# A delta-rule recurrence on one core: the block inverse widened ahead of the value stage, a third RH tile, and 64-row products that alternate between heads

## The chip, the cores and the metric

The kernel runs on 1 of the 8 cores of a Trainium2 chip. The metric is the device time of one execution in microseconds (us). Below, PE is TensorE, DVE is VectorE, ACT is ScalarE, POOL is GpSimd, and SP is SyncE, whose queue issues nearly all DMAs here.

## The reference

One layer of a hybrid decoder trunk, sequence 1024, width 1024. After an RMS norm one projection feeds three mixers: stick-breaking attention (8 heads of 64), a Mamba-2 SSD mixer (16 heads of 64, chunks of 128) and RWKV-7 time mixing (8 heads of 64). Their gated outputs are projected, merged and added to the input. The change lies in the third mixer, whose state `S` (64 x 64 for each head) is stepped through the tokens as

```
sa = S @ (-kk_t)
S  = S * w_t + outer(sa, kk_t * a_t) + outer(v_t, k_t)
y_t = S @ r_t
```

The kernel computes it in chunks of 64 tokens. In each chunk the steps are turned into products of small matrices and one inverse of a unit lower triangular 64 x 64 matrix for each head.

## The kernel before, in words

Everything that PE does is written out in one order by a small planner (`Driver`, lines 69 to 131). It keeps a clock of its own that every product advances by a fixed cost (`Counted`, lines 50 to 66), and at each step it takes the first of the small generators whose yielded pause is over, whose condition holds and whose PSUM banks the plan holds to be free; where there is none, it issues the next piece of a long projection (`proj`, line 243: 24 groups of three fp32r products `pj` of 128x512, hi and lo parts, each with its weights). Projections that nothing waits for, those of the merge gates, are `spare`: they fill PE's time wherever the recurrence or the SSD chunks have nothing ready, but the last four (`KEEP`) are held back for the time after the SSD chunks. PE then runs that list strictly in order. The order on the other engines is made by the framework's scheduler.

`rwkv()` (line 385) goes through 4 pairs of heads. For a pair, `prep` (line 457) makes for each half of the sequence (512 tokens) the decayed vectors: `KR` (keys and receptances) and `BK` (the two factors they are multiplied with). `mats` (line 530) then runs one unit, which is 256 tokens of both heads of the pair, so there are 16 units, `u` = 0 to 15, two to a half. A unit goes through these stages:

- keys: 8 products `pma<-KR,BK` (line 546), each with 64 rows of contraction, in the upper or the lower half of the partitions according to the head; DVE masks them into the tile `RH` (line 548); 4 transposes of `BK` (line 555) complete it;
- a 16 x 16 inverse on DVE for 32 small blocks at once: `RH` goes to DRAM (`dC`, line 563) and comes back as `CB` (line 567); 30 short operations (lines 571 and 573); then out to DRAM as `img` (line 578) and back as the block diagonal tiles `Ta` and `Tb` (line 579);
- value stage (lines 591 to 606): centred values and transposed keys, then 64x64 products with the two heads in opposite quarters of the array;
- widening of the inverse from 16 to 32 (lines 613 to 623: products `Ta,C`, a copy on ACT to `U`, products `Tb,tmp`, a subtraction on DVE to `T32`);
- solving (lines 626 to 642: `X,T`, `tmp,C`, `tmp,T`), operators `Z` (lines 645 to 657), four state steps (line 666) in which a unit needs the state that the unit before leaves, and the normalised output.

What holds a unit back: `mats` starts when `u - 2` has its operators (line 534); the value stage starts when `u - 1` has them (line 590); the widening waits until the plan's clock stands `INV` past the end of the keys stage (line 612). `RH`, `Ta`, `Tb` and `BK` have two buffers each, `T32` one.

Behind the recurrence come the SSD chunks (`ssd()`, line 735). Two groups of 8 chunks are a chain: `first(c)` makes two decay products (`DH,lsr` and `DL,lsr`), from which ACT and DVE make `Mt`; after a pause of `SLOT` in the plan, in which projections fill PE, `second(c)` uses `Mt` (line 975). Then come the attention rows, the output projections and the final norm.

Of the kernel before, what the change touches and what calls it, by code (L numbers as in the profile page):

```python
# [8 lines left out]
F32 = mybir.dt.float32  # L9
# [6 lines left out]
P = 128  # L16
# [7 lines left out]
EXPM05 = 0.6065306597126334  # L24
BKB = 2
TAB = 2
# [5 lines left out]
SLOT = 5.6  # L32
INV = 24.0
LAT = 2.0
# [104 lines left out]
def body_(tc, A, out):  # L139
    nc = tc.nc  # L140
    ctx = ExitStack()
    V, G, T, ACT = nc.vector, nc.gpsimd, Counted(nc.tensor), nc.scalar
    drv = Driver(T)
    tt, ts, stt = V.tensor_tensor, V.tensor_scalar, V.scalar_tensor_tensor
    MUL, ADD, SUB = ALU.mult, ALU.add, ALU.subtract
# [8 lines left out]
    def pm(tag="a", hold=0.0):  # L154
        drv.bank(tag, hold)
        return psm.tile([P, HB], F32, name="pm" + tag)
# [210 lines left out]
    for k in range(KT):  # L367
        ps = pm("cab"[k % 3])
# [16 lines left out]
    def rwkv():  # L385
        rc = ExitStack()
        cc = rc.enter_context(tc.tile_pool(name="rcc", bufs=1))
        pr = rc.enter_context(tc.tile_pool(name="rpr", bufs=1))
        ma = rc.enter_context(tc.tile_pool(name="rma", bufs=1))
# [63 lines left out]
        fl = lambda t: t.rearrange("p b l -> p (b l)")  # L453

        ends, opst = {}, [0.0]

        def prep(hp, hf, rT, kT, vT):
# [6 lines left out]
            aa = pr.tile([P, HB], F32, name="aa")  # L464
            ps = pm("a", 2.4)
            T.matmul(ps, lhsT=wup[0:64, cs], rhs=lo[0:64, hs], start=True, stop=True)
            ACT.activation(out=fl(sg), in_=ps, func=AF.Sigmoid, bias=par("rw_w0", hp))
            ps = pm("a", 2.4)
# [26 lines left out]
            V.tensor_copy(out=ivb, in_=inv.rearrange("p (c h) -> p c h", h=2).unsqueeze(3).broadcast_to([P, 4, 2, 64]))  # L495
            yield 4.5, None, "a"
            ips = pm("a", 2.4)
# [8 lines left out]
            KR = pr.tile([P, 4, 4, 64], F32, name="KR", bufs=2)  # L506
            BK = pr.tile([P, 4, 4, 64], F32, name="BK", bufs=BKB)
# [22 lines left out]
        def mats(hp, hf, g):  # L530


            u = 4 * hp + 2 * hf + g
            yield 0.0, lambda: (hp, hf) in made and T.t >= after[hp, hf] and (u < 2 or u - 2 in ends), "a"
            KR, BK, GL, bv, vs = made[hp, hf]
            a0 = 2 * g
            RH = ma.tile([P, 2, 2, 6, 64], F32, name="RH", bufs=2)
            for h in range(2):
                if h:
                    yield 0.0, None, "a"  # L540
                hr = slice(64 * h, 64 * h + 64)
                ps = pm("a", 2.6)
                pv = ps.rearrange("p (a e x) -> p a e x", a=2, e=2)
                for i in range(2):
                    for e in range(2):
                        T.matmul(pv[:, i, e, :], lhsT=fl(BK[hr, a0 + i, 2 * e:2 * e + 2, :]), rhs=KR[hr, a0 + i, e::2, :],
                                 start=True, stop=True)
                tt(out=RH[:, :, h, 1:5, :].rearrange("p a (e b) l -> p a e (b l)", e=2), in0=pv,
                   in1=fl(msk).unsqueeze(1).unsqueeze(1).broadcast_to([P, 2, 2, P]), op=MUL)
            yield 2.0, None, "b"  # L550
            ps = pm("b", 2.0)
            pv = ps.rearrange("p (a e h l) -> p a e h l", a=2, e=2, h=2)
            for i in range(2):
                for e in range(2):
                    T.transpose(out=ps[:, (2 * i + e) * P:(2 * i + e + 1) * P], in_=fl(BK[:, a0 + i, 2 - 2 * e:4 - 2 * e, :]),
                                identity=ident)
            for i in range(2):
                ACT.copy(out=RH[:, i, :, 0::5, :].rearrange("p h e l -> p e h l"), in_=pv[:, i])
# [15 lines left out]
            V.tensor_copy(out=TX, in_=TB.rearrange("q t j -> q j t"))  # L574
            Ta = ma.tile([P, 4, P], F32, name="Ta", bufs=TAB)
            Tb = ma.tile([P, 4, P], F32, name="Tb", bufs=TAB)
# [6 lines left out]
            for e in range(2):  # L583
                for (cx, mx) in ((C16, m16), (C32, m32)):
                    tt(out=cx[:, :, e, :], in0=RHg[:, :, 2 + 2 * e, :],
                       in1=mx[:, 64 * e:64 * e + 64].unsqueeze(1).broadcast_to([P, 4, 64]), op=MUL)
            f = lambda t, i: fl(t[:, i])

            t0_ = T.t
            yield 2.0, lambda: u == 0 or u - 1 in ends and T.t >= opst[0] + 1.0, "aa"  # L590
# [16 lines left out]

            def tmp():
                return ma.tile([P, 4, P], F32, name="tmp", bufs=2)


            yield max(2.0, INV - (T.t - t0_))
            ups = pm("b")
            for q in range(4):
                T.matmul(ups[:, q * P:(q + 1) * P], lhsT=f(C16, q), rhs=Ta[:, q, :], start=True, stop=True)
            U = tmp()
            ACT.copy(out=fl(U), in_=ups)
            yield LAT
            ups = pm("b")
            for q in range(4):  # L620
                T.matmul(ups[:, q * P:(q + 1) * P], lhsT=U[:, q, :], rhs=Tb[:, q, :], start=True, stop=True)
            T32 = ma.tile([P, 4, P], F32, name="T32")
            tt(out=fl(T32), in0=fl(Tb), in1=ups, op=SUB)

# [49 lines left out]
            for h in range(2):  # L674
                yv = yb[h][:, 0:256].rearrange("p (a e l) -> p a e l", e=2, l=64)
                ACT.copy(out=Yt[0:64, :, h, :], in_=yv[0:64, :, 0, :])
                ACT.copy(out=Yt[64:128, :, h, :], in_=yv[64:128, :, 1, :])
            Yq = ma.tile([P, 4, 64], F32, name="Yq", bufs=2)
            Yt3 = Yt.rearrange("p a h l -> p (a h) l")
# [12 lines left out]
            for i in range(2):  # L692
                T.transpose(out=ps[:, i * P:(i + 1) * P], in_=fl(Yq[:, 2 * i:2 * i + 2, :]), identity=ident)
            yo = pr.tile([P, 256], F32, name="yo", bufs=2)
            t0 = hf * HB + g * 256
# [641 lines left out]
```

## Time and profile before

| what | us |
|---|---|
| median of 3 runs (1584.92 to 1587.72) | 1586.35 |
| the profiled execution | 1585.81 |
| its span in the trace | 1584.1 |
| PE busy | 1546.7 (98%) |
| DVE busy | 966.4 (61%) |
| ACT busy | 724.8 (46%) |
| POOL busy | 214.6 (14%) |

The mean granted PE clock is 0.998 of full speed. A busy time of PE is made of modelled ends, and the records of products that follow each other overlap; so the price of a group of products is read here from the start of its first record to the start of the next group. Each fp32 product leaves two records (a product of 128x128 is two records of 128x128), each fp32r product and each transpose one. Order lists count a product once.

### The profile page before, as it was taken

How to read it: one execution, taken by the hardware profiler on the slowest of the kernel's cores; microseconds unless marked ns; L12 is line 12 of the kernel's file. 1: busy time of each engine (PE TensorE's matmuls, PEld its weight loads, DVE VectorE, ACT ScalarE, POOL GpSimd, SP SyncE). 2: the span in 40 equal slices, each digit the busy share in tenths (PEclk: the TensorE clock that was granted, in tenths of full speed). 3: DMA queues.
4: the chain of work that ended last, by engine and by line, in shares of the span. 5: the costliest groups of instructions: out<-in, count | busy, mean ns of one | idle time of the engine just before them, and what ended most of it. 6: DMA issues, size and time to landing. Idle time of an engine off the chain costs nothing.

```text
span 1584.1 us, 22681 instructions
## 1 busy us (share of the span) xinstructions
PE 1546.7 (98%) x8590; PEld 1256.2 (79%) x8590; DVE 966.4 (61%) x1982; ACT 724.8 (46%) x1212; POOL 214.6 (14%) x321
## 2 busy tenths in 40 slices
PE   7999999999999999999999999999999999999998
PEld 5878877887888788778777777887888778778887
DVE  5375776657567673366987934346574787555623
ACT  6263465546345554454545533246454655321211
POOL 1000000000000000201564620112121311000000
PEclk9999999999999999999999999999999999999999
DMA  4323223122222323201111113511211164886322
GB/s 161 87 61 76 58 78 84 41 62 55 72 56 73 91 51 91 73 27 40 41 41 40 28 41 100 186 44 34 62 34 46 33 207 140 279 287 225 110 107 80
DMA packets 189581, 138.72 MB, mean 88 GB/s; under 512 B 42545, under 2 KB 156320, under 8 KB 189472
## 3 DMA queue, kind: packets, MB, share of 16 engines
q1 hardware_dynamic: 189328, 137.02, 29.0%
q8 instruction: 67, 1.10, 0.3%
q14 instruction: 42, 0.34, 0.1%
q10 hardware_dynamic: 144, 0.26, 0.0%
HBM read 99.50 MB, written 37.75 MB: 87 GB/s over the span
## 4 chain that ended last, share of the span: by engine, by line
PE 80%; DVE 8%; ACT 5%; DMA 4%; issue 2%; SPq 0%; POOL 0%; POOLq 0%; DVEq 0%; ACTq 0%
PE pj L62 51%; PE pmb L62 9%; PE pma L62 9%; PE pmc L62 8%; PE pmb L66 2%; DMA yt<-in_w_o_dram 1%; PE pma L66 1%; DVE wlo L194 1%; DVE kp L1137 1%; ACT whi L193 1%; DVE TX L571 1%; DVE TB L573 1%; DMA yt<-yssd 1%; DMA yt<-ys 1%; DMA wraw<-in_w_in_dram 1%
## 5 line engine op out<-in xcount | busy, mean ns | idle before, releaser
L62 PE MATMUL pj<-hL,whi 128*128 128x512 f32 x1456 | 554.5, 397 | 0.5 <-DVE mo L1219 0.5
L62 PE MATMUL pj<-hH,whi 128*128 128x512 f32 x1328 | 540.4, 415 | 3.3 <-DVE sg L1222 2.2
L62 PE MATMUL pj<-hH,wlo 128*128 128x512 f32 x1264 | 500.3, 396 | 0.5 <-DVE wlo L194 0.5
L62 PEld LDWEIGHTS pj<-hL,whi 128*128 128x128 f32 x1456 | 273.5, 189 | 56.1 <-issue 2.1
L62 PEld LDWEIGHTS pj<-hH,whi 128*128 128x128 f32 x1328 | 250.1, 189 | 64.0 <-issue 8.2
L62 PEld LDWEIGHTS pj<-hH,wlo 128*128 128x128 f32 x1264 | 238.0, 188 | 58.3 <-DVE wlo L194 1.0
L194 DVE TENSOR_TENSOR wlo<-wraw,whi 128x1024 fp32r<-128x1024 f32 x91 | 112.3, 1234 | 153.7 <-ACT whi L193 148.9
L193 ACT CAST whi<-wraw 128x1024 fp32r<-128x1024 f32 x91 | 95.5, 1049 | 182.3 <-PE pj L62 165.6
L1137 DVE TENSOR_TENSOR_SCAN kp<-kp,one 128x127 f32<-128x127 f32 (+7 forms) x64 | 87.8, 1372 | 50.1 <-POOL kp L1135 50.0
L1156 ACT COPY aT<-pmb 128x512 f32<-128x512 f32 (+1 forms) x80 | 41.4, 547 | 57.2 <-PE pmb L66 57.0
L668 DVE TENSOR_SCALAR HI<-pmc,GL 64x64 f32<-64x64 f32 x128 | 32.5, 281 | 55.2 <-PE pmc L62 54.1
L568 POOL TENSOR_SCALAR TB<-id 32x256 f32<-32x256 f32 x16 | 14.8, 924 | 354.0 <-DMA img<-TB 245.1
L1135 POOL TENSOR_SCALAR_AFFINE_SELECT be<-be 128x128 f32<-128x128 f32 x64 | 29.8, 466 | 212.1 <-ACT be L1132 211.7
L1139 DVE TENSOR_TENSOR be<-be,kp 128x127 f32<-128x127 f32 (+7 forms) x64 | 50.0, 781 | 2.8
L62 PE MATMUL pj<-hL,wlo 128*128 128x512 f32 x128 | 50.5, 395 | 0.0
L571 DVE TENSOR_TENSOR TX<-CB,TB 32x15 f32<-32x15 f32 (+7 forms) x240 | 46.3, 193 | 6.7 <-DMA CB<-dC 0.8
L573 DVE TENSOR_TENSOR TB<-TB,TX 32x15 f32<-32x15 f32 (+7 forms) x240 | 46.3, 193 | 6.0
L939 POOL TENSOR_TENSOR DL<-li,d 128x512 fp32r<-128x512 f32 x32 | 45.5, 1434 | 25.5 <-DVE d L855 19.0
L62 PEld LDWEIGHTS pmc<-aT,vt 128*64 128x64 f32 x576 | 30.7, 136 | 16.9 <-ACT kp L1133 6.1
L62 PE MATMUL pmc<-aT,vt 128*64 128x128 f32 x576 | 38.8, 279 | 4.9 <-ACT kp L1133 3.4
L62 PEld LDWEIGHTS pmc<-HI,Z 128*128 128x128 f32 x256 | 37.3, 190 | 7.9 <-ACT Z L657 2.8
L772 DVE SCALAR_TENSOR_TENSOR yc<-pj,pc,yc 128x511 f32<-128x511 f32 (+2 forms) x48 | 35.7, 743 | 8.5 <-ACT yc L770 7.9
(380 smaller groups left out, 2635.7 us busy)
## 6 DMA issues: line engine op xcount, KB each, us to landing
wraw<-in_w_in_dram SPq DMA_DIRECT2D x75, 512.0 KB
sgd<-sgt SPq DMA_DIRECT2D x48, 256.0 KB
sg<-sgd SPq DMA_DIRECT2D x48, 256.0 KB
mg<-mo SPq DMA_DIRECT2D x32, 256.0 KB
mo<-mg SPq DMA_DIRECT2D x32, 256.0 KB
xt<-in_x_dram SPq DMA_DIRECT2D x8, 512.0 KB
Ta<-img SPq DMA_DIRECT2D x16, 256.0 KB
Tb<-img SPq DMA_DIRECT2D x16, 256.0 KB
```

The lines of the kernel that those rows point to most:

```text
L62: return self.eng.matmul(out, lhsT=lhsT, rhs=rhs, **kw)
L66: return self.eng.transpose(**kw)
L193: ACT.copy(out=hi, in_=raw)
L194: tt(out=lo, in0=raw, in1=hi.bitcast(F32), op=SUB)
L571: tt(out=TX[:, j + 1:16, 0:j + 1], in0=CB[:, j, j + 1:16].unsqueeze(2).broadcast_to(sh), in1=TB[:, j:j + 1, 0:j + 1].broadcast_to(sh), op=MUL)
L573: tt(out=TB[:, j + 1:16, 0:j + 1], in0=TB[:, j + 1:16, 0:j + 1], in1=TX[:, j + 1:16, 0:j + 1], op=SUB)
L668: ts(out=HIs[h][cur[h]][0:64, :], in0=o[hr], scalar1=GL[hr, 4 * g + c, h:h + 1], scalar2=None, op0=MUL)
L772: stt(out=o[:, d:], in0=ps[:, 0:HB - d], scalar=w(3 - d), in1=o[:, d:], op0=MUL, op1=ADD)
L939: G.tensor_tensor(out=DL, in0=lb, in1=dal[:, c, h0:h0 + 4].unsqueeze(2).broadcast_to([P, 4, P]), op=MUL)
L1137: V.tensor_tensor_scan(out=kp[:, n - 1:0:-1], data0=kp[:, n - 1:0:-1], data1=one.broadcast_to([P, n - 1]), initial=1.0, op0=MUL, op1=MUL)
L1139: tt(out=be[:, 0:n - 1], in0=be[:, 0:n - 1], in1=kp[:, 1:n], op=MUL)
L1156: ACT.copy(out=aT[:, 0:2 * m, :].rearrange("p x t -> p (x t)"), in_=ps[:, :2 * m * P])
```

## The change

- `BK` has one buffer instead of two. `prep` now waits, before it writes `BK`, until the transposes of the unit before are in the plan (`turned`).
- `RH` has three buffers, and keys may be made when `u - 3` has its operators, one unit sooner.
- The 8 products of the keys stage are written in another order: for each of the four blocks, head 0 and then head 1, into two PSUM banks taken together. The plan's clock is set back by 0.9 behind them.
- The widening stands ahead of the value stage, so it no longer waits for unit `u - 1`; its pause `INV` is 29 instead of 24. `Ta` has one buffer instead of two, `T32` two instead of one.
- `Yq` and `yo` have one buffer instead of two.

No operation is added or removed.

```
-BKB = 2
+BKB = 1
-INV = 24.0
+INV = 29.0
...
-            yield 4.5, None, "a"
+            yield 4.5, lambda: 4 * hp + 2 * hf == 0 or 4 * hp + 2 * hf - 1 in turned, "a"
...
-            yield 0.0, lambda: (hp, hf) in made and T.t >= after[hp, hf] and (u < 2 or u - 2 in ends), "a"
+            yield 0.0, lambda: (hp, hf) in made and T.t >= after[hp, hf] and (u < 3 or u - 3 in ends), "aa"
...
-            RH = ma.tile([P, 2, 2, 6, 64], F32, name="RH", bufs=2)
+            RH = ma.tile([P, 2, 2, 6, 64], F32, name="RH", bufs=3)
+            pvs = [pm("a", 2.8 + 0.7 * h).rearrange("p (a e x) -> p a e x", a=2, e=2) for h in range(2)]
+            for i in range(2):
+                for e in range(2):
+                    for h in range(2):
+                        hr = slice(64 * h, 64 * h + 64)
+                        T.matmul(pvs[h][:, i, e, :], lhsT=fl(BK[hr, a0 + i, 2 * e:2 * e + 2, :]), rhs=KR[hr, a0 + i, e::2, :],
+                                 start=True, stop=True)
+            T.t -= 0.9
             for h in range(2):
-                if h:
-                    yield 0.0, None, "a"
-                hr = slice(64 * h, 64 * h + 64)
-                ps = pm("a", 2.6)
...
+            turned.add(u)
...
-            Ta = ma.tile([P, 4, P], F32, name="Ta", bufs=TAB)
+            Ta = ma.tile([P, 4, P], F32, name="Ta", bufs=1)
...
+            yield INV, None, "b"
+            ups = pm("b", 2.0)
+            for q in range(4):
+                T.matmul(ups[:, q * P:(q + 1) * P], lhsT=f(C16, q), rhs=Ta[:, q, :], start=True, stop=True)
+            U = tmp()
+            ACT.copy(out=fl(U), in_=ups)
+            yield LAT, None, "b"
...
+            T32 = ma.tile([P, 4, P], F32, name="T32", bufs=2)
+            tt(out=fl(T32), in0=fl(Tb), in1=ups, op=SUB)
             yield 2.0, lambda: u == 0 or u - 1 in ends and T.t >= opst[0] + 1.0, "aa"
...
-            yield max(2.0, INV - (T.t - t0_))
...
-            Yq = ma.tile([P, 4, 64], F32, name="Yq", bufs=2)
+            Yq = ma.tile([P, 4, 64], F32, name="Yq")
...
-            yo = pr.tile([P, 256], F32, name="yo", bufs=2)
+            yo = pr.tile([P, 256], F32, name="yo")
```

Two places show how the lists of the engines move. The first is where the inverses of units 0 and 1 come back. On SP, before: the `img` writes of unit 1 (names `img_447`, `img_448`) and the loads of its `Ta` and `Tb`, with what each waits for.

```order
51 L578 DMA img_447<-TB 32x16x16 [waits DMAHW5_49,DVE_49,Pool_49]
52 L578 DMA img_448<-TX 32x16x16 [waits DMAHW6_49,DVE_49]
53 L579 DMA Ta<-img_447 128x4x128 [waits DMAHW5_49]
54 L579 DMA Tb<-img_448 128x4x128 [waits DMAHW6_49]
55 L192 DMA wraw<-in_w_in_dram 128x8x128 [waits DMAHW3_49,DMAHW1_49,DVE_49]
```

On SP, now:

```order
54 L580 DMA img_447<-TB 32x16x16 [waits DVE_49,Pool_49]
55 L580 DMA img_448<-TX 32x16x16 [waits DMAHW1_49,DVE_49]
56 L192 DMA wraw<-in_w_in_dram 128x8x128 [waits DMAHW2_49,DVE_49]
57 L581 DMA Ta<-img_447 128x4x128 [waits DMAHW3_49,DMAHW0_49,PE_49]
58 L581 DMA Tb<-img_448 128x4x128 [waits DMAHW4_49,DMAHW1_49]
59 L580 DMA img_445<-TB 32x16x16 [waits DVE_49,Pool_49]
```

The load of unit 1's `Ta` now waits for PE, and the `Tb` load and the next unit's `img` write stand behind it. On PE, before: the first widening product `Ta,C` of unit 0 and the rows up to its second one, `Tb,tmp`, with nine projection products between; unit 1's `Ta,C` comes 104 rows on.

```order
469 L62 MATMUL pmb<-Ta,C_973 128x128 x4
470 L62 MATMUL pj<-hH,whi 128x512
471 L62 MATMUL pj<-hL,whi 128x512
472 L62 MATMUL pj<-hH,wlo 128x512
473 L62 MATMUL pj<-hH,whi 128x512
474 L62 MATMUL pj<-hL,whi 128x512
475 L62 MATMUL pj<-hH,wlo 128x512
476 L62 MATMUL pj<-hH,whi 128x512
477 L62 MATMUL pj<-hL,whi 128x512
478 L62 MATMUL pj<-hH,wlo 128x512
479 L62 MATMUL pmb<-Tb,tmp 128x128 x4
```

On PE, now, from `Ta,C` of unit 0 (`C_982`) to that of unit 1 (`C_1071`):

```order
492 L62 MATMUL pmb<-Ta,C_982 128x128 x4
493 L62 MATMUL pj<-hH,whi 128x512
494 L62 MATMUL pj<-hL,whi 128x512
495 L62 MATMUL pj<-hH,wlo 128x512
496 L62 MATMUL pj<-hH,whi 128x512
497 L62 MATMUL pj<-hL,whi 128x512
498 L62 MATMUL pj<-hH,wlo 128x512
499 L62 MATMUL pj<-hH,whi 128x512
500 L62 MATMUL pj<-hL,whi 128x512
501 L62 MATMUL pj<-hH,wlo 128x512
502 L62 MATMUL pmb<-Tb,tmp 128x128 x4
503 L62 MATMUL pmb<-Ta,C_1071 128x128 x4
```

The second widening begins right behind the first, with nine projection products and `Tb,tmp` between the two reads of the one `Ta` buffer. The second place is the end of the SSD chunks. On PE, before: from the decay products of the last chunk but one to those of the last, 27 projection products lie ahead of the `EAx` row; here are the last rows of that filler, `second(6)`, `first(7)` and the beginning of `second(7)`.

```order
3241 L62 MATMUL pj<-hH,wlo 128x512
3242 L62 MATMUL pmb<-EAx,sel 128x512
3243 L62 MATMUL pmc<-cT,St_6278 128x128 x4
3244 L62 MATMUL pmc<-xw,bt 128x512
3245 L62 MATMUL pma<-Mt,xd 64x128 x8
3246 L62 MATMUL pma<-cT,bz_6280 128x128
3247 L62 MATMUL pmb<-DH,lsr 128x512
3248 L62 MATMUL pmb<-DL,lsr 128x512
3249 L62 MATMUL pmb<-DH,lsr 128x512
3250 L62 MATMUL pmb<-DL,lsr 128x512
3251 L62 MATMUL pj<-hH,whi 128x512
```

On PE, now, from the end of `first(6)` to that of `first(7)`:

```order
3242 L62 MATMUL pmb<-DL,lsr 128x512
3243 L62 MATMUL pmb<-EAx,sel 128x512
3244 L62 MATMUL pmc<-cT,St_6340 128x128 x4
3245 L62 MATMUL pmc<-xw,bt 128x512
3246 L62 MATMUL pma<-Mt,xd 64x128 x8
3247 L62 MATMUL pma<-cT,bz_6342 128x128
3248 L62 MATMUL pmb<-DH,lsr 128x512
3249 L62 MATMUL pmb<-DL,lsr 128x512
3250 L62 MATMUL pmb<-DH,lsr 128x512
3251 L62 MATMUL pmb<-DL,lsr 128x512
3252 L62 MATMUL pmb<-EAx,sel 128x512
```

No projection product stands in the last two chunks any more. On DVE, now, what stands there from the last chunk but one on (`yc` is the addition of a chunk's output, `St` the state):

```order
1457 L978 TENSOR_TENSOR yc<-pma,yc 128x4x128
1458 L973 TENSOR_TENSOR St_6340<-St_6340,pmc 64x512
1459 L947 TENSOR_TENSOR cb<-pma,li 128x128
1460 L948 TENSOR_TENSOR xd<-xt,dt 128x512
1461 L951 TENSOR_TENSOR Mt<-Mt,cb 128x512
1462 L939 TENSOR_TENSOR DH<-li,dah 128x512
1463 L951 TENSOR_TENSOR Mt<-Mt,cb 128x512
```

On DVE, before, the same stretch:

```order
1471 L971 TENSOR_TENSOR St_6278<-St_6278,pmc 64x512
1472 L977 TENSOR_TENSOR yc<-pma,yc 128x4x128
1473 L946 TENSOR_TENSOR cb<-pma,li 128x128
1474 L950 TENSOR_TENSOR Mt<-Mt,cb 128x512
1475 L194 TENSOR_TENSOR wlo<-wraw,whi 128x1024
1476 L950 TENSOR_TENSOR Mt<-Mt,cb 128x512
```

The last `DH`, which PE's second pair of decay products needs, now stands between the two `Mt`.

## Rows read from the trace of the kernel before

**Rows 1.** The page, part 1: busy us (share of the span) xinstructions of each engine.

```profile
PE 1546.7 (98%) x8590; PEld 1256.2 (79%) x8590; DVE 966.4 (61%) x1982; ACT 724.8 (46%) x1212; POOL 214.6 (14%) x321
```

**Rows 2.** Windows: stretch and length; PE, PEld, DVE, ACT, POOL busy; granted clock; DMA.

```profile
100.00:640.00 540.00, 528.65 (x3291) 444.43 (x3292) 351.83 (x1111) 270.41 (x450) 15.75 (x27) 1.00 0.26 68
```

**Rows 3.** Groups by form, 100 to 700 us: xrecords | busy us, mean ns | idle before.

```profile
L62 PE MATMUL pma<-KR,BK 64*128 64x128 f32 x256 | 28.6, 285 | 0.2 <-ACT sg L467 0.2
```

**Rows 4.** Timeline of PE, one keys stage and what follows: start, us, what, records.

```profile
385.01 1.71 PE L62 MATMUL pma<-KR,BK 64*128 64x128 f32 x16
386.64 0.50 PE L62 MATMUL pj<-hH,whi 128*128 128x512 f32 x1
```

**Rows 5.** Timeline of PE: 64-row products in both halves; one full 128-row product.

```profile
99.86 1.13 PE L62 MATMUL pma<-lo,wup 64*128 64x512 f32 x4
100.92 0.50 PE L62 MATMUL pj<-hH,whi 128*128 128x512 f32 x1
...
395.27 1.02 PE L62 MATMUL pma<-kp,bo 128*128 128x512 f32 x2
396.22 0.27 PE L62 MATMUL pma<-ZLe,RH 64*64 64x64 f32 x1
```

**Rows 6.** Timeline of PE: 64x64 products in opposite quarters of the array.

```profile
396.32 0.22 PE L62 MATMUL pma<-ZLe,RH 64*64 64x64 f32 x1
396.33 0.22 PE L62 MATMUL pma<-ZLo,RH 64*64 64x64 f32 x1
396.38 0.22 PE L62 MATMUL pma<-ZLe,RH 64*64 64x64 f32 x1
```

**Rows 7.** Timeline of PE: short products with full weights; products alternating between output halves.

```profile
429.63 0.55 PE L62 MATMUL pmc<-HI,Z 128*128 128x64 f32 x4
430.00 0.48 PE L62 MATMUL pj<-hH,whi 128*128 128x512 f32 x1
...
902.09 1.09 PE L62 MATMUL pma<-Mt,xd 128*64 128x128 f32 x16
903.12 0.49 PE L62 MATMUL pma<-cT,bz 128*128 128x128 f32 x2
```

**Rows 8.** Chain of waits, a Ta load from issue to landing: start, us, what.

```profile
197.91 2.83 DMA Ta<-img
```

**Rows 9.** Timeline of PE: unit 9's BK transposes.

```profile
389.28 0.60 PE L66 MATMUL pmb<-ident,BK 128*128 128x128 f32 x4
```

**Rows 10.** Timeline of SP: unit 9's Ta load is issued.

```profile
416.86 0.38 SPq L579 DMA_DIRECT2D Ta<-img  x1
```

**Rows 11.** Timeline of PE: nine projection products and a widening product.

```profile
409.64 0.48 PE L62 MATMUL pj<-hH,whi 128*128 128x512 f32 x1
...
411.83 1.05 PE L62 MATMUL pmb<-Tb,tmp 128*128 128x128 f32 x8
412.64 0.48 PE L62 MATMUL pj<-hH,whi 128*128 128x512 f32 x1
```

**Rows 12.** Chain of waits, filler of the last two SSD chunks.

```profile
904.55 6.29 PE pj L62 x27
...
915.21 0.47 PE pj L62 x2
```

**Rows 13.** Timeline of PE, last SSD chunk: [idle before <-releaser].

```profile
918.68 0.66 PE L62 MATMUL pma<-Mt,xd 128*64 128x128 f32 x8 [0.98 <-DVE Mt L950]
```

**Rows 14.** Timeline of DVE, SSD chunks.

```profile
885.26 0.78 DVE L947 TENSOR_TENSOR xd<-xt,dt 128x512 f32<-128x512 f32 x1
...
898.23 1.28 DVE L950 TENSOR_TENSOR Mt<-Mt,cb 128x512 f32<-128x512 f32 x2
...
905.63 0.68 DVE L938 TENSOR_TENSOR DH<-li,dah 128x512 fp32r<-128x512 f32 x1
...
914.29 0.69 DVE L977 TENSOR_TENSOR yc<-pma,yc 128x512 f32<-128x512 f32 x1
914.90 0.28 DVE L946 TENSOR_TENSOR cb<-pma,li 128x128 f32<-128x128 f32 x1
```

More of the change, by code (lines that the diff above doesn't have):

```diff
@@ L453, in rwkv @@
         fl = lambda t: t.rearrange("p b l -> p (b l)")
-        ends, opst = {}, [0.0]
+        ends, opst, turned = {}, [0.0], set()
         def prep(hp, hf, rT, kT, vT):
@@ L533, in mats @@
             u = 4 * hp + 2 * hf + g
-            yield 0.0, lambda: (hp, hf) in made and T.t >= after[hp, hf] and (u < 2 or u - 2 in ends), "a"
+            yield 0.0, lambda: (hp, hf) in made and T.t >= after[hp, hf] and (u < 3 or u - 3 in ends), "aa"
             KR, BK, GL, bv, vs = made[hp, hf]
             a0 = 2 * g
-            RH = ma.tile([P, 2, 2, 6, 64], F32, name="RH", bufs=2)
-            for h in range(2):
-                if h:
-                    yield 0.0, None, "a"
-                hr = slice(64 * h, 64 * h + 64)
-                ps = pm("a", 2.6)
[L543 to L547, printed above, removed]
+            RH = ma.tile([P, 2, 2, 6, 64], F32, name="RH", bufs=3)
[7 more added lines that the diff above has]
+            T.t -= 0.9
+            for h in range(2):
+                pv = pvs[h]
                 tt(out=RH[:, :, h, 1:5, :].rearrange("p a (e b) l -> p a e (b l)", e=2), in0=pv,
                    in1=fl(msk).unsqueeze(1).unsqueeze(1).broadcast_to([P, 2, 2, P]), op=MUL)
-            yield 2.0, None, "b"
+            yield 1.5, None, "b"
             ps = pm("b", 2.0)
@@ L587, in mats, with tmp @@
             f = lambda t, i: fl(t[:, i])
-            t0_ = T.t
+            def tmp():
+                return ma.tile([P, 4, P], F32, name="tmp", bufs=2)
+            yield INV, None, "b"
[5 more added lines that the diff above has]
+            yield LAT, None, "b"
+            ups = pm("b", 2.2)
+            for q in range(4):
+                T.matmul(ups[:, q * P:(q + 1) * P], lhsT=U[:, q, :], rhs=Tb[:, q, :], start=True, stop=True)
+            T32 = ma.tile([P, 4, P], F32, name="T32", bufs=2)
+            tt(out=fl(T32), in0=fl(Tb), in1=ups, op=SUB)
             yield 2.0, lambda: u == 0 or u - 1 in ends and T.t >= opst[0] + 1.0, "aa"
@@ L606, in mats @@
             ACT.copy(out=X.rearrange("p q k l -> p k q l"), in_=xps.rearrange("p (k q l) -> p k q l", k=2, q=4))
-            def tmp():
-                return ma.tile([P, 4, P], F32, name="tmp", bufs=2)
-            yield max(2.0, INV - (T.t - t0_))
[L613 to L623, printed above, removed]
             yield LAT
```

## The prediction

> **What bounds the kernel now.** I read the page first, for which engine is full. PE is busy for 98% of the span, every other engine for 61% or less [rows 1]. The windows then say whether the recurrence, where the change lies, is an exception: from 100 to 640 us PE is busy for 528.65 of 540 us, at a granted clock of 1.00 [rows 2]. So the recurrence does not wait for its own chain of small products. Projections fill every pause, and PE stands still for only 540 - 528.65 = 11.35 us in the whole stretch. What the kernel costs is the time of PE's list plus the few waits in it. A shorter chain for a unit is therefore worth nothing by itself. An edit can act in three ways: it shortens PE's list, it removes some of those 11.35 us, or it makes a new wait. That is the frame for all that follows.
>
> **The change part by part.** *64-row products.* A keys stage leaves 16 records (8 products), and from its start to the start of the next product it takes 386.64 - 385.01 = 1.63 us [rows 4], 102 ns a record. The group has 256 records, so there are 16 such stages [rows 3]. The products use half the rows of the array, first all of one half, then all of the other. Does the array run two halves side by side when they alternate? Three rows of before bear on it. Two products of 64 rows and 512 columns, one in each half, take 100.92 - 99.86 = 1.06 us, while a single product of the same columns on all rows takes 396.22 - 395.27 = 0.95 us [rows 5]: two for little more than the price of one. The 64x64 products in opposite quarters start 0.01 us apart, and the next pair 0.06 us after the first [rows 6]. Both speak for it. The third, products that alternate between halves of the output columns, has 16 records in 903.12 - 902.09 = 1.03 us [rows 7]; these also have 128 columns to stream, so this is the nearest row for an overlap that is not complete. Full overlap would give 1.63 / 2 = 0.82 us. I take 0.88, nearer to the full overlap because [rows 5] has exactly this geometry: a saving of 0.75 us for a unit, **12.0 us** for 16. The bounds are 13.0 us (0.82) and 0 (no overlap); a loss is excluded, since the same products in the same two banks at worst go one after the other.
>
> What could spoil it is the loading of weights, 128 columns for each record. [Rows 7] also bounds that: products with 128 columns of weights and only 64 to stream take (430.00 - 429.63) / 4 = 92 ns a record, though half the streaming should take half of 102. So loading seems to set a floor near 92 ns where loads come one after another. In [rows 6], with half the columns, that floor would be 46 ns a record and 92 ns a pair; the pair takes 60, so there loads run side by side too.
>
> The Trainium skill has a rule for either side. In TensorE: Matmul & The Clock Gate, section "LDWEIGHTS (loading the stationary operand)", loading goes by columns alone, P / 1.2 ns, whatever the rows; by it 16 loads one after another would be an estimated 16 x 107 = 1.71 us, no gain at all. The same page, Part 3, section "The mechanism", lets a load run beside running products when its row group is another one, which would give about half of today's time; the trace's pairs 60 ns apart [rows 6] agree with the second, and no run so far shows 128 columns in each half.
>
> *Filler moves out of the SSD chunks.* The order has 590 groups of three projection products ahead of the transposes at line 826, the first of the SSD mixer, and 606 after the change: the recurrence takes 16 groups more. They are missing in the SSD chunks (136 groups as filler before, 120 after). PE's sum stays the same, but four gates are held back there, so nothing replaces them. The last chunk of the first group keeps 4 of 9 groups, one chunk 8 of 9, and the last two have none, where before the last but one had 9 and the last had 1. A filled chunk has 27 products in 6.29 us; the small products take 915.21 - (904.55 + 6.29) = 4.37 us [rows 12]. What does a chunk without filler wait for? For DVE. Before, the last chunk with one group of filler stood still for 0.98 us until `Mt` came [rows 13]. In the last chunk now, DVE has ahead of the last `DH`, in the order shown: `yc` 0.69, `St` (taken like `yc`) 0.69, `cb` 0.28, `xd` 0.78, one `Mt` 0.64, and `DH` itself 0.68 [rows 14], 3.76 us from the end of the chunk before; PE has about 0.8 us of short products to do first (an estimate: `cT,bz` and the first decay pair out of the 4.37). That is a stall of 3.0 us, 2.0 more than before. For the last chunk but one the list is `yc`, `cb`, `DH`, two `Mt`, 0.69 + 0.28 + 0.68 + 1.28 = 2.93 us, against some 3.3 of the 4.37 us that PE has ahead of `Mt,xd`: no stall if DVE is undisturbed, 2 us if POOL slows it. I take 1. Together **+3.0 us**, bounds 0 and 7.8 (PE waits as long again as its small products take in both chunks, 2 x 4.37, less the old 0.98).
>
> *The inverse.* Widening earlier changes when the products run, not how many there are. But one `Ta` buffer and early keys bring a new wait. In four pairs of units (0/1, 4/5, 8/9, 12/13) the two widenings stand 9 to 12 projection products and `Tb,tmp` apart. That is 411.83 - 409.64 = 2.19 us plus 412.64 - 411.83 = 0.81 us [rows 11], so 3.0 us for 0/1 and 3.7 us for the others, between the last read of `Ta` and the next `Ta,C`. The load takes 2.83 us from its issue [rows 8], so it just fits when SP is free at once and nothing else is on the queues. Behind the waiting load stand the `Tb` load, the next `img` write, and the weight load of a later projection, which is not needed at once. The second question is whether the second inverse is ready. Unit 9, whose keys came as close behind unit 8's as all four pairs do now, had its `Ta` at 416.86 + 2.83 = 419.69 [rows 8, 10], 30.4 us after its transposes at 389.28 [rows 9]; the plan now allows 29 of its own clock. So a wait of about 0.75 us for each pair: **+3.0 us**, bounds 0 and 12 (3 us each, a whole load).
>
> *The rest.* `RH` with three buffers, `turned`, one `Yq`, `yo` and `BK`: all are gates in the plan or reuse after tens of us, covered by filler, price 0. If a `BK` write did wait, PE would still have projections. Whether the 11.35 us of small waits grow (stages of neighbouring units now bunch) or shrink (two fewer links between values and solution) I cannot read from before: 0, bounds -6 and +6.
>
> **Sum.** Against the profiled execution: 1585.81 - 12.0 + 3.0 + 3.0 + 0 = 1579.8 us. The median of the runs lies 0.54 above that execution, so **1580 us**, 0.4% less.
>
> **The rivals.** *The waits fall too.* The full 13.0 us come, half of the 11.35 us goes because the solution has fewer links, and pairs and chunks cost 1 us each: 1586.35 - 13.0 - 5.7 + 2 = 1570 us. For it: the old waits lie just in those links. Against it: the same number of products with the same pauses stays, in a tighter stretch.
>
> *The second inverse comes late.* This one ends slower. Place: `Ta,C` of units 1, 5, 9 and 13. Both inverses of a pair go through one `CB` tile and DVE one after the other, while the next half's vectors are made, and then the second load waits for PE besides. Where it comes 4.5 us late, PE stands still behind a product that heads its list: 4 x 4.5 = 18 in place of 3: 1586.35 - 12 + 3 + 18 = 1595 us. It decides from 12.2 us in all (12.0 - 3.0 + 3.2), so from 3.0 us a pair. For it: 30.4 against 29, and no buffer is left. Against it: in the other pairs of before the keys lay further apart and each inverse was early.
>
> *The halves do not overlap.* Loads bound them at 92 ns: 16 x 92 = 1.48 us instead of 1.63, 2.4 us saved in all: 1586.35 - 2.4 + 3 + 3 = 1590 us. For it: [rows 7]. Against it: [rows 5, 6]. In this case the change doesn't do what it says.
>
> **How the numbers follow.** The forecast 0.60, with its own range 1575 to 1586; waits fall 0.15; late inverse 0.13; no overlap 0.12. About 0.2% (3.2 us) is what a measurement of this kernel can tell from no change. Faster by more than that means below 1583.2: 0.47 of the forecast's 0.60 and the 0.15 make 0.62. Slower, above 1589.5: 0.10 of the late inverse and 0.06 of no overlap make 0.16. The rest, 0.22, is within it. The range is 1571 to 1591: it leaves out the lower half of the first rival and the worse part of the second.
>
> **What would show it.** Right: the 16 records of a keys stage take 0.82 to 1.03 us to the next product, with records of the two halves starting together; small waits on `Mt` and `DH` in the last two SSD chunks; a wait under 1.5 us at `Ta,C` of units 1, 5, 9, 13; PE idle between 100 and 640 us within 6 us of 11.35. Wrong: keys stages still at 1.5 us or more; a wait of 3 us or more at those `Ta,C`; new waits in the solving stages; or a stall over 5 us in the SSD chunks.

## The result, and the profile after

The changed kernel takes 1604.29 us (median of 4 runs, 1601.72 to 1608.05) against 1586.15 us before in the same set of runs: a ratio of 1.0116, 95% interval 1.0092 to 1.0139. It is slower by some 18 us where 6 us less was forecast. The profiled executions are 1601.72 and 1585.81 us, with spans of 1600.0 and 1584.1; the 15.9 us between the two spans are what is taken apart here. The profiled execution of the changed kernel is the fastest of its four. Every ratio below leaves out one slow run of the kernel before, which took 3065.5 us.

Part 1 of the page, PE and DVE alone of interest, answers to [rows 1]:

```profile
PE 1544.3 (97%) x8590; PEld 1250.0 (78%) x8590; DVE 965.9 (60%) x1982; ACT 728.5 (46%) x1215; POOL 215.2 (13%) x321
```

PE has as many instructions as before and is busy for 2.4 us less, in a span 15.9 us longer. So the work did not grow; PE waits more. (ScalarE's three instructions more are table loads, 100 instead of 97, though the kernel text adds no operation.) Where PE waits, the windows say, the same stretch as [rows 2]:

```profile
100.00:640.00 540.00, 517.50 (x3257) 431.44 (x3256) 346.60 (x1099) 272.70 (x450) 16.18 (x26) 0.99 0.26 68
```

PE stands still for 540 - 517.50 = 22.50 us, 11.35 before, and the granted clock has fallen below 1.00. The keys products answer to [rows 3, 4], first the group, then one stage on PE's timeline:

```profile
L62 PE MATMUL pma<-KR,BK 64*128 64x128 f32 x256 | 19.1, 285 | 1.2 <-ACT inv L491 1.2
```

```profile
103.88 1.16 PE L62 MATMUL pma<-KR,BK 64*128 64x128 f32 x16
104.97 0.50 PE L62 MATMUL pj<-hH,whi 128*128 128x512 f32 x1
```

The stage takes 104.97 - 103.88 = 1.09 us instead of 1.63: the halves do overlap, and in full. The kernel before shows it where the plan put projections between the two heads, so that one head's 8 records stand alone:

```profile
281.02 1.16 PE L62 MATMUL pma<-KR,BK 64*128 64x128 f32 x8
282.10 0.50 PE L62 MATMUL pj<-hH,whi 128*128 128x512 f32 x1
```

One head alone takes 282.10 - 281.02 = 1.08 us, and both heads in turn take 1.09. So two separate heads cost 2.16 us, and the 1.63 of [rows 4] already held an overlap: where the heads follow each other directly, the second adds 1.63 - 1.08 = 0.55 us and not 1.08. What PE waits for instead, 100 to 655 us (engine, tile, line <- releaser: us in total, times, longest):

```profile
PE pmc L66 <- DVE Yq L686: 3.7, 2, 1.9
PE pma L62 <- ACT ZLe L615: 2.8, 2, 2.1
PE pmb L62 <- DMA Ta<-img: 2.5, 3, 1.5
PE pmc L62 <- ACT Z L658: 2.4, 3, 1.5
PE pmb L62 <- DVE TB L575: 2.1, 3, 1.7
PE pma L66 <- DVE sq L495: 2.0, 1, 2.0
PE pma L66 <- DVE TB L575: 1.8, 1, 1.8
PE pma L62 <- DVE TX L573: 1.6, 1, 1.6
PE pma L62 <- ACT inv L491: 1.2, 1, 1.2
```

The second inverse, about which the prediction worried, is the third line, 2.5 us in all; the worst single one is on the timeline of PE:

```profile
282.24 1.13 PE L62 MATMUL pmb<-Ta,C 128*128 128x128 f32 x8 [1.47 <-DMA Ta<-img]
```

The others are a crowd of small waits on ScalarE and VectorE. The kernel before had its longest on ScalarE, and few on VectorE:

```profile
PE pmb L62 <- ACT tmp L630: 4.7, 2, 3.0
PE pmb L62 <- DVE tmp L636: 1.9, 5, 0.6
```

Added up by releaser over the whole recurrence, the waits on ScalarE are 8.8 us before and 8.5 after, those on VectorE 2.9 and 12.0, those on `Ta` 0 and 2.5. So the growth is in the waits on VectorE; those on ScalarE have only moved. One of each kind shows how they come about. First VectorE: PE writes the input of `tmp` (line 637) in the group from 319.55, then runs six projection products and stands still before it can use the result.

```profile
319.55 1.05 PE L62 MATMUL pmb<-tmp,C 128*128 128x128 f32 x8
...
324.61 1.13 PE L62 MATMUL pmb<-tmp,T 128*128 128x128 f32 x8 [1.72 <-DVE TB L575]
```

VectorE in that time:

```profile
320.08 1.21 DVE L194 TENSOR_TENSOR wlo<-wraw,whi 128x1024 fp32r<-128x1024 f32 x1
...
322.35 0.71 DVE L288 SCALAR_TENSOR_TENSOR f<-pj,pc,f 128x511 f32<-128x511 f32 x1
...
323.80 0.67 DVE L637 TENSOR_TENSOR tmp<-X,pmb 128x512 f32<-128x512 f32 x1
```

The group that writes the input gives way to the next one at 320.44, but `tmp` starts at 323.80, behind the rows of another unit's inverse, its masks and the conversion of projection weights. Then ScalarE's timeline, and what PE does at that time:

```profile
353.77 0.58 ACT L658 COPY Z<-pmb 64x512 f32<-64x512 f32 x1
354.38 0.69 ACT L470 ACTIVATE aa<-pma,pc 128x512 f32<-128x512 f32 x1
355.08 1.28 ACT L475 ACT_TABLE_LOAD   x1
356.38 0.63 ACT L475 ACTIVATE E<-sg 128x512 f32<-128x512 f32 x1
357.03 1.28 ACT L313 ACT_TABLE_LOAD   x1
358.32 0.60 ACT L313 ACTIVATE sgt<-pj 128x512 f32<-128x512 f32 x1
358.94 1.28 ACT L477 ACT_TABLE_LOAD   x1
360.23 0.63 ACT L477 ACTIVATE sg<-sg 128x512 f32<-128x512 f32 x1
360.88 0.37 ACT L615 COPY ZLe<-pma 64x256 f32<-64x256 f32 x1
```

```profile
361.30 0.47 PE L62 MATMUL pma<-ZLe,RH 64*64 64x64 f32 x2 [2.11 <-ACT ZLe L615]
```

A unit's value stage now meets the vectors of the next half. The copy that PE needs stands at the end of a full ScalarE queue: three table loads of 1.28 us and four activations. Behind this wait the granted clock (the third number from the end in a window) is at its lower level, 0.50:

```profile
355.00:361.00 6.00, 4.19 (x26) 3.55 (x24) 3.97 (x14) 5.89 (x8) 0.00 (x0) 1.00 0.11 44
361.30:368.10 6.80, 6.80 (x38) 6.29 (x39) 2.30 (x7) 2.91 (x5) 0.00 (x0) 0.50 0.00 0
```

Then the end of the SSD mixer, where the filler is missing. PE's timeline, with the idle time before a row and its releaser in brackets, answers to [rows 13]:

```profile
917.65 0.50 PE L62 MATMUL pmb<-EAx,sel 128*128 128x512 f32 x1 [0.85 <-ACT Mt L945]
...
919.40 1.12 PE L62 MATMUL pmc<-xw,bt 128*128 128x512 f32 x2 [0.36 <-DVE yo L967]
924.72 1.97 PE L62 MATMUL pma<-Mt,xd 128*64 128x128 f32 x16 [4.20 <-DVE Mt L951]
926.62 0.80 PE L62 MATMUL pma<-cT,bz 128*128 128x128 f32 x2
...
930.68 0.47 PE L62 MATMUL pmb<-DH,lsr 128*128 128x512 f32 x1 [2.53 <-DVE DH L939]
```

PE waits 0.85 + 0.36 + 4.20 + 2.53 = 7.94 us here, against 0.98 in [rows 13]. DVE's and POOL's rows of the longest wait answer to [rows 14]:

```profile
920.05 1.77 DVE L939 TENSOR_TENSOR DH<-li,dah 128x512 fp32r<-128x512 f32 x1
921.75 3.42 DVE L951 TENSOR_TENSOR Mt<-Mt,cb 128x512 f32<-128x512 f32 x2
```

```profile
920.02 1.26 POOL L980 TENSOR_TENSOR yc<-yc,yo 128x512 f32<-128x512 f32 x1 [0.50 <-DVE yc L978]
921.24 2.78 POOL L1005 TENSOR_TENSOR acc<-acc,zs 128x1024 f32<-128x1024 f32 x1
```

`DH` takes 1.77 us where [rows 14] has 0.68, and the two `Mt` 3.42 where it has 1.28: together 3.23 us longer. POOL works from 920.02 to 924.02, and both of its additions lie on top of just these instructions. The numbers fit one engine standing until the other's instruction is through: from 921.75 to POOL's end at 924.02 are 2.27 us, and 2.27 + 1.28 = 3.55. The Trainium skill has the rule in SBUF — State Buffer, section "SBUF: two separate sides": a VectorE instruction with two SBUF inputs and a GpSimd instruction that reads SBUF take one port pair, for a whole instruction, and the later one blocks. This trace agrees, and the engine that came first was not slowed: POOL's `yc` took 1.26 us here and 1.28 at 927.50. The kernel before has such a pair too, `Mt` with 3.22 us at 887.41; there filler hid it.

At both waits the clock then falls as well:

```profile
924.50:927.90 3.40, 3.18 (x20) 2.53 (x20) 3.10 (x6) 0.00 (x0) 0.40 (x1) 0.50 0.00 0
931.30:934.70 3.40, 3.40 (x22) 3.08 (x22) 1.39 (x2) 2.36 (x3) 0.00 (x0) 0.50 0.02 5
```

The `Mt,xd` products, 16 records, take 926.62 - 924.72 = 1.90 us instead of the 1.03 of [rows 7].

**The ledger.** I sum PE's records from one start to the next, from the first keys product to the first `zs` transposes, and keep the idle time apart. This is the recurrence.

| us, profiled execution | before | after | difference |
|---|---|---|---|
| start of the first keys product | 102.5 | 103.9 | +1.4 |
| keys products (256 records) | 27.3 | 17.9 | -9.4 |
| waits of PE in the recurrence | 11.7 | 23.0 | +11.2 (2.5 of it on `Ta`) |
| projections in the recurrence | 349.8 | 359.4 | +9.6 |
| its other products | 181.9 | 185.4 | +3.5 |
| SSD chunks, `DH,lsr` to `acc,on` | 227.8 | 227.3 | -0.5 |
| `zs` transposes to `DH,lsr` | 72.2 | 72.2 | 0 |
| after `acc,on` | 610.8 | 611.0 | +0.2 |

Of the 16 groups of projections that moved forward, one lies ahead of the first keys product. A group costs 6.29 / 9 = 0.70 us [rows 12], so 16 are 11.2 us. That leaves the recurrence with 1.4 - 9.4 + 11.2 + 9.6 + 3.5 - 11.2 = +5.1 us of its own. The chunks, which took nearly the old time with 11.2 us less to do, have lost 11.2 - 0.5 = +10.7 us.

### The profile page after: what moved, and what is told of

Its sections match the earlier page's. It is cut to its first block, busy times and chain, and to the rows that moved or that the text cites. A ratio compares the mean times of both kernels' runs of the same rounds, so it can differ in the third digit from the quotient of the medians.

```text
span 1600.0 us, 22721 instructions
## 1 busy us (share of the span) xinstructions
PE 1544.3 (97%) x8590; PEld 1250.0 (78%) x8590; DVE 965.9 (60%) x1982; ACT 728.5 (46%) x1215; POOL 215.2 (13%) x321
## 4 chain that ended last, share of the span: by engine, by line
PE 75%; DVE 11%; DMA 6%; ACT 4%; issue 3%; SPq 0%; POOL 0%; POOLq 0%; DVEq 0%; ACTq 0%
PE pj L62 48%; PE pmb L62 9%; PE pma L62 8%; PE pmc L62 7%; PE pmb L66 2%; DVE TB L575 1%; DVE TX L573 1%; DMA yt<-in_w_o_dram 1%; PE pma L66 1%; DVE kp L1138 1%; DVE wlo L194 1%; DMA wraw<-in_w_in_dram 1%; DMA img<-TB 1%; DMA yt<-yssd 1%; DMA Ta<-img 1%
## 5 line engine op out<-in xcount | busy, mean ns | idle before, releaser
L62 PEld LDWEIGHTS pj<-hH,whi 128*128 128x128 f32 x1328 | 250.0, 189 | 67.0 <-issue 12.2
```

Source lines behind the costliest of these rows:

```text
L62: return self.eng.matmul(out, lhsT=lhsT, rhs=rhs, **kw)
```

## Experiments

Four kernels share one set of runs of before (1585.53 us), the next four a second (1586.13), the last two a third (1585.91). Medians of different sets can be half a microsecond apart for that reason alone, so kernels of different sets are compared by ratio too. Two small parts of the change, the plan's clock set back by 0.9 and a pause of 1.5 instead of 2.0 ahead of the transposes of `BK`, stand in e2, e3 and e8 only, and no run takes them alone. "Waits" and "keys products" mean the rows of the ledger.

**e1, the alternating heads alone**, in the kernel before; the stage asks for one bank of the pool as before.

```
+            pvs = [pm("a", 2.8 + 0.7 * h).rearrange("p (a e x) -> p a e x", a=2, e=2) for h in range(2)]
+            for i in range(2):
+                for e in range(2):
+                    for h in range(2):
+                        hr = slice(64 * h, 64 * h + 64)
+                        T.matmul(pvs[h][:, i, e, :], lhsT=..., rhs=..., start=True, stop=True)
```

> The kernel before with one part of the change alone: the 8 products of a keys stage alternate between the heads, in two banks. Theory (PE is full, so what its list loses the span loses): a keys stage falls from 1.64 us to the 1.09 us that it takes in the changed kernel, 27.3 us to 17.5 us for all 16, so 1586.15 - 9.8 = 1576 us (1574 to 1580). Rival (the time is given back, since the results that PE waits for next come no earlier): keys stages at 1.09 us, but 1584 to 1588 us.

Measured: 1581.70 us, ratio 0.9979 (0.9970 to 0.9987). Keys products 18.8 us, -8.5. The waits grow by 2.4 (14.15), most of it one new wait, on the reader of the second bank:

```profile
PE pma L62 <- DVE RH L547: 1.8, 1, 1.8
```

The overlap is real and makes the kernel faster by 4 us. Of the 8.5 us, 2.4 go into these waits, and in the profiled executions 1.3 into projections of the recurrence that take longer and 1.0 into the stretch behind the chunks. Neither forecast held.

**e2, the change without the alternation**: all else of the change, heads one after the other.

```
-            for i in range(2):
-                for e in range(2):
-                    for h in range(2):
+            for h in range(2):
+                for i in range(2):
+                    for e in range(2):
```

> The changed kernel with the products of a keys stage written head after head again, everything else as changed, PE's list otherwise the same row for row. Theory: each of 16 stages is 0.55 us longer, so 1604.3 + 8.8 = 1613 us (1609 to 1617). Rival (the waits hide it): 1602 to 1607 us.

Measured: 1608.47 us, ratio 1.0149 (1.0136 to 1.0163); keys products 26.8, waits 20.2. The same saving from the other side: 26.8 - 17.9 = 8.9 us of the list, 2.8 us more waits, 4.2 us at the median (8.6 between the profiled executions; the runs of the two kernels overlap, so the size is rough). The time lies just under the theory's range. The loss is in the rest of the change, 23 us of it.

**e3, the change with the SSD chunks filled as before.** KEEP is the number of projection groups that the planner holds back; three make the 16 groups come back into the chunks.

```
-KEEP = 4
+KEEP = 3
```

> The changed kernel with one gate fewer held back (KEEP 3), so that the SSD chunks have the same filler as in the kernel before, 9 groups in each and 1 in the last. The recurrence is that of the changed kernel. Theory (the missing filler costs what the stage took longer, 10.7 us, with the granted clock that falls behind its waits): 1604.3 - 10.7 = 1594 us (1591 to 1597), and no half clock in the chunks. Rival (as forecast, missing filler costs 3 us and the rest of the loss there comes from DVE's other order): 1600 to 1602 us.

Measured: 1595.32 us, ratio 1.0068 (1.0050 to 1.0085), 9.0 us less than the change at the median, 7.6 by the ratios. The theory held: no half clock in the chunks, and only the old wait is left there:

```profile
PE pma L62 <- DVE Mt L951: 1.0, 1, 1.0
```

**e4, the kernel before with the same 16 groups missing** in its chunks (KEEP 5), nothing else changed.

```
-KEEP = 4
+KEEP = 5
```

> The kernel before with one gate more held back (KEEP 5), so that the SSD chunks lack the same 16 groups as in the changed kernel: 4 in the last chunk of the first group, 8, 0 and 0 at the end. The recurrence is untouched. Theory: the stage alone costs 10.7 us more, 1586.15 + 10.7 = 1597 us (1594 to 1600), with the granted clock at half for some us at the end of the chunks. Rival (as forecast): 3 us, 1589 us (1587 to 1591).

Measured: 1600.19 us, ratio 1.0098 (1.0085 to 1.0112). PE's timeline has the same two waits as the changed kernel, with the same releasers:

```profile
907.64 1.98 PE L62 MATMUL pma<-Mt,xd 128*64 128x128 f32 x16 [4.20 <-DVE Mt L950]
...
913.60 0.47 PE L62 MATMUL pmb<-DH,lsr 128*128 128x512 f32 x1 [2.39 <-DVE DH L938]
```

From `DH,lsr` to `acc,on` it takes 227.1 us, 0.7 less than before with 11.2 us of filler gone: the chunks lose 10.5 us with the recurrence untouched. The filler now runs behind them, where the stretch to the end grows by 16.2 us, 5.0 more than the filler itself, which puts the total just above the theory's range. So some 8 to 11 us of the change's loss is the missing filler, shown from both sides, and my 3 us for it is refuted.

**e5, the widening ahead of the values alone**, with the old allowance for the inverse (INV 24); `T32` has two buffers, `Yq` and `yo` one.

```
+            yield INV, None, "b"
+            ups = pm("b", 2.0)
...
             yield 2.0, lambda: u == 0 or u - 1 in ends and T.t >= opst[0] + 1.0, "aa"
...
-            yield max(2.0, INV - (T.t - t0_))
-            ups = pm("b")
```

> The kernel before with the widening moved ahead of the value stage alone (T32 two buffers, Yq and yo one; INV stays 24, keys, RH, BK and Ta as before). The recurrence takes as many groups of filler as before, so the SSD chunks are filled as before. The order of the changed recurrence, without missing filler, costs 9.8 us (e3 against before) although its keys stages are 8 to 9 us shorter, so 14 to 18 us of waits and half clock are new there. Theory (the widening of one unit now falls on the preparation of the next half and on the value stage of the unit before, on ACT and DVE): this part carries most, 1585.5 + 10 = 1595 us (1591 to 1600). Rival (the early keys with one BK carry it): 1584 to 1589 us.

Measured: 1619.24 us, ratio 1.0214 (1.0200 to 1.0228). PE waits 36.3 us in the recurrence, most of it in one line:

```profile
PE pmb L62 <- DMA Ta<-img: 24.3, 6, 8.1
```

Without the value stage ahead of it the widening reaches PE before the inverse is back. Both forecasts missed, since neither had this wait.

**e6, the early keys alone**: the `turned` gate, three `RH`, one `BK`, one `Yq` and `yo`.

```
-BKB = 2
+BKB = 1
-            yield 4.5, None, "a"
+            yield 4.5, lambda: 4 * hp + 2 * hf == 0 or 4 * hp + 2 * hf - 1 in turned, "a"
-            ... (u < 2 or u - 2 in ends), "a"
+            ... (u < 3 or u - 3 in ends), "a"
-            RH = ma.tile([P, 2, 2, 6, 64], F32, name="RH", bufs=2)
+            RH = ma.tile([P, 2, 2, 6, 64], F32, name="RH", bufs=3)
```

> The kernel before with the early keys alone: RH three buffers, keys from u - 3, BK one buffer with the wait for the transposes, Yq and yo one; widening, INV and the order of the heads as before, SSD filler as before. Theory (see e5): this part carries little, 1585.5 + 2 = 1588 us (1584 to 1591). Rival: it carries most, 1595 us (1591 to 1600).

Measured: 1594.43 us, ratio 1.0054 (1.0041 to 1.0066). Waits 16.0, +4.2, here behind copies of the widening and of the solution:

```profile
PE pmb L62 <- ACT tmp L618: 5.4, 2, 4.9
PE pmb L62 <- ACT ZLo L643: 4.6, 3, 1.8
```

Edits that I had priced at nothing cost 8 us by themselves, as the rival said. The keys products take 2.2 us more as well: in six stages instead of two the heads are apart, at 2.16 us for 1.63.

**e7, e1 with KEEP 3.**

```
-KEEP = 4
+KEEP = 3
```

> Alternating heads alone (e1) with KEEP 3, so that all 16 SSD chunks have 9 groups of filler; that gate is then missing later. Theory: the last wait for Mt (0.98 us) goes, the rest stays: 1581 us (1579 to 1583). Rival (as in e3, where the stages behind the chunks took 2.4 us more than the 16 missing groups explain, the gate is worth more later): 1583 to 1587 us.

Measured: 1584.87 us, ratio 0.9992 (0.9983 to 1.0001), 3.2 us behind e1 at the median, 2.1 by the ratios, as the rival said. The chunks gain 1.3 us, but behind `acc,on` the time falls by 7.6 us only, with 11.2 us of filler fewer. More filler held for the chunks is not free either: it is missing later.

**e8, the change with INV 24.**

```
-INV = 29.0
+INV = 24.0
```

> The changed kernel with INV 24 again. The recurrence gets 16 groups shorter, so the SSD chunks are filled as before: - 9 us. But the plan lets each widening come 5 us sooner. In the changed kernel the Ta of units 1, 5, 9 and 13 landed about when its product stood at the head of PE's list (it waited 2.5 us in all), and the others had 5 us and more to spare. Theory (PE then waits for the second inverse of each pair): + 4 x 4.5, so 1604 - 9 + 18 = 1613 us (1607 to 1619), with waits of 3 us and more on Ta. Rival (DVE and SP get to the second inverse as much sooner as the plan does): 1593 to 1597 us.

Measured: 1612.36 us, ratio 1.0173 (1.0157 to 1.0189). The recurrence takes no more filler than before and the chunks are full, but:

```profile
PE pmb L62 <- DMA Ta<-img: 17.5, 3, 7.4
PE pmb L62 <- DVE TX L573: 7.2, 3, 3.1
```

The theory held. With 24 the inverse comes too late, with 29 it does not (nothing between was run), and the 16 groups are what the 5 us cost. One buys the other.

**e9, the widening ahead alone, with INV 29**, and KEEP 1, which keeps the chunks full but for 13 of 672 products. `T32`, `Yq` and `yo` are as in e5.

```
-INV = 24.0
+INV = 29.0
-KEEP = 4
+KEEP = 1
...
+            yield INV, None, "b"
+            ups = pm("b", 2.0)
```

> The kernel before with the widening ahead of the values alone, now with INV 29 as the change has it (two Ta buffers, heads one after the other, keys not early), and KEEP 1 so that the SSD chunks stay filled as before; the gate at the vT transposes then lies 16 groups later, as in the version of the change with KEEP 3. With INV 24 the same edit took 1619 us with 24.3 us of waits on Ta. Theory: those waits came from INV alone, and the change's remaining +9 to +10 us with filled chunks are the early keys (+8 by themselves) and the later gate (+3): so here the waits on Ta fall under 5 us and the time is 1588 to 1592, before + 3 for the gate and 0 to 3 for the widening. Rival: moving the widening ahead bunches the stages of neighbouring units in any case and costs 8 us or more by itself: 1597 or later, PE's waits between the first keys and the zs transposes at 20 us or more (before: 11.7).

Measured: 1609.95 us, ratio 1.0152 (1.0138 to 1.0166). In the recurrence the theory held: waits 14.15 us, +2.4, and on the inverse almost none,

```profile
PE pmb L62 <- DMA Ta<-img: 0.5, 1, 0.5
```

but it takes 48 groups more, which cost 34.2 of the 36.4 us by which it is longer. The rest of the loss comes much later, at 1024 us, in one wait, with the granted clock low around it:

```profile
PE pj L62 <- DVE Qs L1071: 13.6, 1, 13.6
```

```profile
1000.00:1050.00 50.00, 36.45 (x148) 28.43 (x147) 25.98 (x21) 13.12 (x17) 2.55 (x5) 0.86 0.51 174
```

So its total tells nothing of the widening. The theory missed the time, and the rival, whose time it reached, missed the waits (20 us or more). What made `Qs` late stays open.

**e10, e1 with both banks asked for**, to be rid of its new wait.

```
-            ... (u < 2 or u - 2 in ends), "a"
+            ... (u < 2 or u - 2 in ends), "aa"
```

> The alternating heads alone, with the gate asking for both of the first pool's banks to be free before the keys stage begins (the earlier run of the heads alone, at 1581.7 us, asked for one, and PE stood 1.8 us behind the second bank's last reader). Theory: the overlap of 16 stages of about 9 us then comes to the end in full but for half a microsecond a stage: 1577 to 1580. Rival: the packing's saving is partly given back by other waits, since the stage only comes sooner to what DVE and ScalarE release: 1581 to 1584, like the version with one bank asked for.

Measured: 1584.74 us, ratio 0.9993 (0.9984 to 1.0002). The wait on `RH` did not go (3.0 us, twice), others came, 17.4 us in all, and from 100 to 640 us the mean clock is 0.98 instead of e1's 1.00; but the profiled execution, 1588.44 us, is the slowest of its eleven. Neither forecast held. Keys products 18.3 us, as good as in e1, and the gain is gone at the end. e1 remains the fastest version: 0.2% ahead of before, 1.4% ahead of the change.

## Why the prediction was wrong

**The frame was right**: PE's list, the old waits, new waits. Two of four terms came out beyond their bounds, the filler and the rest, both on the side of new waits. The forecast was -6.0 us and the trace has +15.9: the keys products give 2.6 us less than said, the filler costs 7.7 more, the inverse 0.5 less, the other waits 8.7, and 3.4 us, products that ran slower for the most part, were in no term.

**64-row products, -12.0.** The mechanism is right, the size was too large: 1.09 us a stage, outside the 0.82 to 1.03 forecast, and -9.4 us in all. The step that failed here is the price of full overlap, 1.63 / 2 = 0.82 us. It took the 16 records of [rows 4] to stand one after the other, but one head alone takes 1.08 us and two apart 2.16, so full overlap is 1.08 and saves 27.3 - 16 x 1.08 = 10.0 us at most. The rows at 281.02 us of the kernel before had it. The rival without overlap is refuted by e1 and e2.

**Filler moves out of the SSD chunks, +3.0, bounds 0 and 7.8.** This step failed: +10.7 in the trace, +7.6 to +9.0 by e3, +10.5 by e4. The direction and the engine were right. I priced the chunk before the last at 1 us because DVE's rows there sum to less than PE's small products, with 2 us if POOL slowed it. POOL did, by 3.23 us, since its addition to `acc` falls into this chunk and the estimate left it out; without these 3.23 us the wait of 4.20 would be 0.97, the 1 that I took. The last chunk's 2.53 us is near the 3.0 forecast. The upper bound also failed, since it held waits only: waits grew by 7.94 - 0.98 = 7.0 us, and the other 3.7 are products that ran slower, for which the trace offers the two stretches at half clock (some 3 us by the price worked out below).

**The inverse, +3.0.** Right: 2.5 us, the longest 1.47, no pair near the 3.0 us at which the rival would have decided. The rival "the second inverse comes late" named 1595 us but not for what happened; e8 shows that it would have come true with INV 24, with 20.6 us of waits at the four places that it named. What I did not follow is the price of the 29: the longer plan is the reason that the recurrence takes the 16 groups, so this term and the one before it are one decision.

**The rest, 0, bounds -6 and +6.** This step failed too. The waits not on `Ta` grew by 11.2 - 2.5 = 8.7 us. I priced these edits at nothing because PE would still have projections. It does, but a stage that heads PE's list waits all the same, however much filler stands behind it. Each part by itself adds waits, the heads 2.4 us (e1), the early keys 4.2 (e6), the widening 2.4 (e9), but the 9.0 are not the change's waits in pieces. The change's growth is on VectorE (2.9 to 12.0 us), and the waits on it are 4.7, 1.6, 0.7 and 2.8 us in e1, e6, e5 and e9; in the kernels that have the early keys and the widening together they are 11.8 (e2), 12.2 (e3) and 13.4 (e8). So it takes the two together, with the small edits that come with them. That small stages stand in VectorE's queue behind another unit's inverse is read from one place of the trace, and from one on ScalarE, which is full there (5.89 of 6 us in the window from 355 us); for the other waits it is argued. The rival in which the old waits fall is refuted: the old ones on `tmp` did go (4.7 us before, 0.3 after), and others came for them.

**What was not in the sum**: the granted clock. Before, it fell once in this stretch, for 3.4 us; in the changed kernel it is at 0.50 for 6.8 us behind the `ZLe` wait and twice 3.4 us in the chunks. What such a fall costs can be read from before and e4: PE's list in the recurrence is the same row for row and the waits are 11.7 and 11.8 us, but e4 has no fall there and takes 569.3 us instead of 570.8. So 3.4 us at half clock cost some 1.5 us, and of the recurrence's +3.5 us of slower products about that much is the longer fall; the rest stays open. Both have the same wait of 3.0 us at this place, so a wait of that length does not always bring a fall.

Of the signs named beforehand, PE's idle time more than 6 us off 11.35 and new waits in the solving stages (1.72 us ahead of `tmp,T`) are in the trace. The stall over 5 us in the chunks is there only as a sum, 4.20 and 2.53 us.

## What to carry to other kernels

Where PE is 98% busy with filler, the filler is a budget: an edit that makes one stretch longer takes it from another, so price the stretch that loses it by running the old kernel with that filler taken away, as e4 did. A chain of small stages is not free because PE has projections left; look at which engine's queue the next stage's input stands in, and what else that engine has in these 5 us. And when a DVE stall is estimated, lay POOL's rows beside DVE's before adding up undisturbed durations.

## What the runs showed of the hardware

- Products of 64 rows and 128 columns in opposite halves of the array overlap in full when they alternate: 16 records in 1.09 us, where the 8 of one half alone take 1.08. Half after half they take 1.63 us, since the second half starts before the first is through.
- VectorE's `Mt` and `DH` are 2.6 to 2.7 times as long (3.42 against 1.28 us, 1.77 against 0.68) while POOL adds tensors.
- After waits of PE of 2.1 to 4.2 us the granted clock lay at 0.50, 1.2 GHz, for 3.4 or 6.8 us: `Mt,xd` took 1.90 us there instead of 1.03. A wait of 3.0 us was followed by a fall in the kernel before and by none in e4, at the same place of the same list; the fall cost some 1.5 us.
- Two versions with the same filler and nearly the same keys products (e1 and e10) lie 3.0 us apart at the median, 2.2 by the ratios. Here the small waits are worth as much as the edit.
